# Fox and dilated attention: the 128-column products as three float32r matmuls, and the gate's tokens streamed in turn

## The chip, the cores and the metric

The kernel runs on one core of one Trainium2 chip. The metric is the device time of one execution in microseconds (us), the median of three runs; lower is better.

## What is computed

A decoder trunk of two layers on 256 tokens of width 2048, all in float32. Layer 0 is "forgetting" attention (fox, 16 heads of 128), layer 1 a mixture of three dilated causal windows (8 heads, values of 256); each is followed by a squared-ReLU MLP of width 8192.

```
q = rms_norm(q, q_gain); k = rms_norm(k, k_gain)
c = cumsum(log_sigmoid(h @ w_f + b_f))
s = q @ k.T * scale + c[query] - c[key];  s[key > query] = -inf
o = softmax(s) @ v                       # fox, per head
...
s_g = q_g @ k_g.T * scale - slope * distance * r_g   # dilated, g = 0, 1, 2
o = sum_g exp(s_g - m) @ v / sum_g den_g
x = x + o @ w_out;  x = x + relu(h @ w_up)**2 @ w_down
```

## The kernel before

**Matmuls.** Weights stream from HBM in pieces of 128x1024. ScalarE casts each piece to a float32r "high" part (`wh`, L398) and VectorE subtracts to get the "low" part (`wl`, L399), five pieces ahead at most (`W_BUFS`). Activations are split in the same way. A float32 product is then three float32r matmuls into one PSUM bank: high by high, high by low, low by high (L447 to L449). `in_turn` makes the moving operand alternate between the two halves of a row's columns, element by element; the products that come out are read back through `by_column`.

**Order.** The program is written as one stream: `product_steps` emits the six matmuls of a weight row block and calls `jobs.tick()`, and jobs written as generators (`qk_chain`, `v_chain`, `fox_head`, `dil_head`, `gate_chain`) put their instructions in between; a `yield n` in a job means n steps later. `pin` fixes that order on every engine.

**Attention.** The 256 tokens are two blocks of 128. For queries of block 0 only keys of block 0 count: 128 columns. For block 1 both do: 256 columns. `scores` makes both: for t = 0 one plain float32 matmul of 128 columns on unsplit operands (L797), for t = 1 three float32r matmuls of 256 columns (L800). `pv` multiplies values by the turned probabilities: the values of key block 0 by 256 columns as three float32r matmuls (L749), those of key block 1 by 128 columns as one float32 matmul (L748). `qk_chain` writes q and k with their gains (L707), splits them (L714, L718), and leaves the block-0 queries whole. `v_chain` writes the values (L725, L726) and the low part of block 0's (L728). `p_split` splits the first 256 columns of the probabilities (L775, L777). There are 16 fox heads with one call of `scores` for each t and one step of `pv` each, and 8 dilated heads with three calls of `scores` for each t and two steps of `pv` each.

**The gate.** `gate` multiplies the forget columns (32 stationary columns, high and low) by the normed tokens' high and low parts, 512 contiguous columns, in 16 float32r matmuls (L811), between two projections of layer 0; `gate_chain` reads the sum.

Of the kernel before, what the change touches and what calls it, by code (L numbers as in the profile page):

```python
# [119 lines left out]
def trunk(ctx: ExitStack, tc, x, fox_w_in, fox_b_f, fox_q_gain, fox_k_gain, fox_w_out, dil_w_in,  # L120
# [303 lines left out]
    def halves(t, apart=NC // 2):  # L424
        return t.rearrange("p (b h n) -> p b h n", n=apart, h=2)
# [238 lines left out]
    def qk_chain(acc, tag, key, parts):  # L664
# [35 lines left out]
        yield clear(6)  # L700
        for t in range(NT):
            subs = []
            for n, (c, nh, gcol, (whole, hi, lo)) in enumerate(parts):
                keys = hi.shape[2] == S
                src = qn[t].rearrange("p i (h r) -> p h i r", h=4)[:, c // P:c // P + nh]
                to = sq[0].rearrange("p (n i x) -> p n i x", n=2, i=2)[:, n] if t else whole
                nc.scalar.activation(to.rearrange("p h (i r) -> p h i r", i=4), src, AF.Copy, scale=gain[:, gcol:gcol + 1])  # L707
                if t == 0 and not keys:
                    continue
                at = slice(t * P, (t + 1) * P) if keys else slice(0, P)  # L710

                a, b = (x[:, :, at].rearrange("p i (h n) -> p i h n", h=2) for x in (hi, lo))
                of = to.rearrange("p i (n h) -> p i h n" if keys else "p i (h n) -> p i h n", h=2)
                nc.scalar.copy(a, of)  # L714
                subs.append((b, of, a))
            yield 2
            for b, of, a in subs:
                nc.vector.tensor_sub(b, of, a.bitcast(F32))  # L718
        jobs.done.add(key)

    def v_chain(acc, tag, key, dst):
        yield (tag, "rstd")
        whole, v_hi, v_lo = dst
        by_rstd = [rstd[tag][:, t:t + 1] for t in range(NT)]
        nc.scalar.activation(halves(v_hi), by_column(acc[0]), AF.Copy, scale=by_rstd[0])  # L725
        nc.scalar.activation(halves(whole), by_column(acc[1]), AF.Copy, scale=by_rstd[1])  # L726
        yield 1
        nc.vector.scalar_tensor_tensor(halves(v_lo), by_column(acc[0]), by_rstd[0], halves(v_hi).bitcast(F32),  # L728
                                       ALU.mult, ALU.subtract)
        jobs.done.add(key)  # L730

    oT = {}
# [1 line left out]


    def by_token(po):
        return po[:, 0:S].rearrange("p (n b) -> p b n", b=2)

    def pv(pt_sb, vt, cols, o_hi, o_lo, name, apart):
        for i, c in enumerate(cols):  # L740
            if i:
                yield 1
            po = ps_sc.tile([P, 512], F32, tag="sc", name=f"po_{name}_{i}")
            whole, v_hi, v_lo = vt
            p_hi, p_lo, p_whole = pt_sb
# [4 lines left out]
            hi, lo = (o.rearrange("p (b n) -> p b n", b=2) for o in (o_hi[i], o_lo[i]))  # L750
# [17 lines left out]
        return turned  # L768

    def p_split(turned, name):  # L770
        both = work.tile([P, 2, S], F32R, tag="pT", name=f"pT_{name}", bufs=1)
        p_hi, p_lo = both[:, 0], both[:, 1]
        first = turned.rearrange("p i b r -> p b i r")[:, 0:2]
        hi, lo = (x.rearrange("p (b i r) -> p b i r", b=2, i=4) for x in (p_hi, p_lo))
# [3 lines left out]
        return p_hi, p_lo, turned[:, :, 2, :]  # L778

    def heads_pairs(name, slot):  # L780


        whole = work.tile([P, 2, 2, P], F32, tag=f"qkw{slot}", name=f"{name}w", bufs=1)
        q = work.tile([P, 2, 2, P], F32R, tag=f"q{slot}", name=f"{name}q", bufs=1)
        k = [work.tile([P, 2, S], F32R, tag=f"k{x}{slot + 3}", name=f"{name}k{x}", bufs=1) for x in "hl"]
        return (whole[:, 0], q[:, 0], q[:, 1]), (whole[:, 1], *k)

    def values(name):
        whole = work.tile([P, NC], F32, tag="vw", name=f"{name}w", bufs=1)
# [17 lines left out]
    def gate(tag):  # L807
        pf = ps_sc.tile([2 * FH, 2 * S], F32, tag="sc", name="pf")
        for k in range(KC):
            both = hT[tag][k // 2][:, k % 2]  # L810
            nc.tensor.matmul(pf, wfs[:, k, :], both.rearrange("p x s -> p (x s)"), start=k == 0, stop=k == KC - 1)  # L811
        jobs.spawn(gate_chain(tag, pf))

    def gate_chain(tag, pf):
# [8 lines left out]
        nc.vector.tensor_copy(f, pf[:, 0:S])  # L823
        nc.vector.tensor_add(f, f, pf[:, S:2 * S])
        yield 3
        pft = ps_sc.tile([P, NT, 2 * FH], F32, tag="sc", name="pft")
        for t in range(NT):
            nc.tensor.transpose(pft[:, t, :], f[:, t * P:(t + 1) * P], ident[:2 * FH, :2 * FH])
        z = small.tile([P, NT, FH], F32, tag="g_z", name="g_z", bufs=1)
# [23 lines left out]
        lf = small.tile([P, NT, FH], F32, tag="g_lf", name="g_lf", bufs=1)  # L853
# [468 lines left out]
```

## Time and profile before

| what | value |
|---|---|
| median of 3 runs | 2083.81 us (2083.33 to 2084.59) |
| span of the profiled execution | 2081.4 us |
| PE (TensorE matmul) busy | 2076.2 us, 100% |
| PEld (TensorE weight load) busy | 1819.9 us, 87% |
| DVE (VectorE) busy | 1714.8 us, 82% |
| ACT (ScalarE) busy | 1306.1 us, 63% |
| DMA, mean | 259 GB/s |

The span runs from the first to the last instruction of the profiled execution. Its own device time is not listed apart from the runs; the runs' median is 2.4 us above the span, which is the start and the end that lie outside it. A matmul's row gives its start and its modelled end, through the array's pipeline; what a matmul costs in a stream is therefore the distance from its start to the next one's, not its duration. A plain float32 matmul shows as two records (x2), each with a weight load.

### The profile page before, as it was taken

How to read it: one execution, taken by the hardware profiler on the slowest of the kernel's cores; microseconds unless marked ns; L12 is line 12 of the kernel's file. 1: busy time of each engine (PE TensorE's matmuls, PEld its weight loads, DVE VectorE, ACT ScalarE, POOL GpSimd, SP SyncE). 2: the span in 40 equal slices, each digit the busy share in tenths (PEclk: the TensorE clock that was granted, in tenths of full speed). 3: DMA queues.
4: the chain of work that ended last, by engine and by line, in shares of the span. 5: the costliest groups of instructions: out<-in, count | busy, mean ns of one | idle time of the engine just before them, and what ended most of it. 6: DMA issues, size and time to landing. Idle time of an engine off the chain costs nothing.

```text
span 2081.4 us, 28973 instructions
## 1 busy us (share of the span) xinstructions
PE 2076.2 (100%) x9838; PEld 1819.9 (87%) x9838; DVE 1714.8 (82%) x2183; ACT 1306.1 (63%) x1825; POOL 275.1 (13%) x398
## 2 busy tenths in 40 slices
PE   9999999999999999999999999999999999999999
PEld 7888888888888888888888888888888888888888
DVE  6888876898989889888668787766998898899874
ACT  6665654866666667664656565556766676666662
POOL 2000000111212112120010010000113031212120
PEclk9999999999999999999999999999999999999999
DMA  8888887888988898897877876867888888898885
GB/s 258 257 259 261 262 249 213 268 284 265 270 282 265 263 299 272 264 286 246 281 242 230 250 238 211 262 212 236 269 275 264 279 274 266 276 288 277 263 277 168
DMA packets 357205, 539.04 MB, mean 259 GB/s; under 512 B 43752, under 2 KB 144448, under 8 KB 357056
## 3 DMA queue, kind: packets, MB, share of 16 engines
q1 hardware_dynamic: 334624, 507.41, 76.6%
q0 software_dynamic: 22016, 29.38, 6.2%
q8 instruction: 77, 1.26, 0.2%
q10 hardware_dynamic: 416, 0.39, 0.1%
q14 instruction: 72, 0.59, 0.1%
HBM read 484.09 MB, written 40.39 MB: 252 GB/s over the span
## 4 chain that ended last, share of the span: by engine, by line
PE 98%; DVE 1%; ACT 1%; DMA 1%; issue 0%; SPq 0%; ACTq 0%
PE acc L447 26%; PE acc L448 26%; PE acc L449 26%; PE wide_n_tp L1140 2%; PE wide_n_tp L1141 2%; PE wide_n_tp L1142 2%; PE wide_n_sc L1141 2%; PE wide_n_acc L1140 2%; PE wide_n_sc L1140 2%; PE wide_n_acc L1142 2%; PE wide_n_sc L1142 2%; PE wide_n_acc L1141 2%; PE sc_d L800 0%; DVE wl L399 0%; DMA turned_n<-blocks_n 0%; PE sc_f L800 0%
## 5 line engine op out<-in xcount | busy, mean ns | idle before, releaser
L399 DVE TENSOR_TENSOR wl<-raw,wh 128x1024 fp32r<-128x1024 f32 (+1 forms) x763 | 919.9, 1215 | 302.4 <-ACT wh L398 295.2
L398 ACT CAST wh<-raw 128x1024 fp32r<-128x1024 f32 (+1 forms) x763 | 787.3, 1046 | 498.9 <-PE acc L449 370.1
L447 PE MATMUL acc<-wh,hT_n 128*128 128x512 f32 x1280 | 486.3, 380 | 0.0
L448 PE MATMUL acc<-wl,hT_n 128*128 128x512 f32 x1280 | 485.3, 379 | 0.2 <-DVE wl L399 0.2
L449 PE MATMUL acc<-wh,hT_n 128*128 128x512 f32 x1280 | 485.2, 379 | 0.0
L449 PEld LDWEIGHTS acc<-wh,hT_n 128*128 128x128 f32 x1280 | 241.9, 189 | 34.4 <-DVE hT_n L631 0.2
L448 PEld LDWEIGHTS acc<-wl,hT_n 128*128 128x128 f32 x1280 | 242.1, 189 | 33.7 <-DVE wl L399 0.9
L447 PEld LDWEIGHTS acc<-wh,hT_n 128*128 128x128 f32 x1280 | 242.1, 189 | 33.0 <-ACT hT_n L630 0.2
L447 PE MATMUL acc<-wh,aTh_n1a 128*128 128x512 f32 x512 | 194.0, 379 | 0.0
L448 PE MATMUL acc<-wl,aTh_n1a 128*128 128x512 f32 x512 | 194.0, 379 | 0.0
L449 PE MATMUL acc<-wh,aTl_n1a 128*128 128x512 f32 x512 | 194.0, 379 | 0.0
L447 PE MATMUL acc<-wh,aTh_n3a 128*128 128x512 f32 x480 | 181.9, 379 | 0.0
L448 PE MATMUL acc<-wl,aTh_n3a 128*128 128x512 f32 x480 | 181.9, 379 | 0.0
L449 PE MATMUL acc<-wh,aTl_n3a 128*128 128x512 f32 x480 | 181.9, 379 | 0.0
L996 POOL DMA_DIRECT2D x<-y_n x96 | 84.7, 1325 | 480.0 <-ACT y_n L995 421.1
L398 ACT CAST wh<-sd 128x1024 fp32r<-128x1024 f32 x80 | 84.1, 1051 | 101.9 <-DVE sd L395 78.5
L398 ACT CAST wh<-v 128x1024 fp32r<-128x1024 f32 x80 | 84.1, 1052 | 53.8 <-PE acc L449 41.4
L448 PEld LDWEIGHTS acc<-wl,aTh_n1a 128*128 128x128 f32 x512 | 96.8, 189 | 13.8
L449 PEld LDWEIGHTS acc<-wh,aTl_n1a 128*128 128x128 f32 x512 | 96.8, 189 | 13.7
L447 PEld LDWEIGHTS acc<-wh,aTh_n1a 128*128 128x128 f32 x512 | 96.8, 189 | 13.7
L399 DVE TENSOR_TENSOR wl<-v,wh 128x1024 fp32r<-128x1024 f32 x80 | 97.5, 1218 | 5.8 <-ACT wh L398 4.5
L395 DVE TENSOR_TENSOR sd<-raw,raw 128x1024 f32<-128x1024 f32 x80 | 97.4, 1218 | 5.5 <-DMA raw<-in_mlp_w_up_dram 5.5
(665 smaller groups left out, 3216.8 us busy)
## 6 DMA issues: line engine op xcount, KB each, us to landing
raw<-in_mlp_w_up_dram SPq DMA_DIRECT2D x296, 512.0 KB, 4.9
raw<-in_mlp_w_down_dram SPq DMA_DIRECT2D x256, 512.0 KB, 5.1
raw<-in_dil_w_in_dram SPq DMA_DIRECT2D x192, 256.0 KB, 3.5
raw<-in_fox_w_in_dram SPq DMA_DIRECT2D x94, 512.0 KB, 5.0
raw<-in_fox_w_out_dram SPq DMA_DIRECT2D x32, 512.0 KB, 4.9
raw<-in_dil_w_in_dram SPq DMA_DIRECT2D x32, 512.0 KB, 5.4
raw<-in_dil_w_out_dram SPq DMA_DIRECT2D x32, 512.0 KB, 4.5
x<-y_n POOLq DMA_DIRECT2D x96, 128.0 KB, 6.2
```

Source lines behind the costliest of these rows:

```text
L395: nc.vector.tensor_sub(quarters[0], raw, raws[n - 1][:, 1, :].unsqueeze(1).to_broadcast([P, RAW_SUB, NC]))
L398: nc.scalar.copy(hi[:, part, :], raw[:, part, :])
L399: nc.vector.tensor_sub(lo[:, part, :], raw[:, part, :], hi[:, part, :].bitcast(F32))
L447: nc.tensor.matmul(acc[t], ah[:, tok], hi, start=first, stop=False)
L448: nc.tensor.matmul(acc[t], ah[:, tok], lo, start=False, stop=False)
L449: nc.tensor.matmul(acc[t], al[:, tok], hi, start=False, stop=last)
L996: nc.gpsimd.dma_start(xt[n][:, t, h * HC:h * HC + HC], y, accum_op=ALU.add)
L1140: nc.tensor.matmul(banks[bank], ah, wh, start=what < 3 and of == 0, stop=False, **alone)
L1141: nc.tensor.matmul(banks[bank], ah, wl, start=False, stop=False, **alone)
L1142: nc.tensor.matmul(banks[bank], al, wh, start=False, stop=of == KC // 2 - 1, **alone)
```

## The change

All 72 plain float32 products of 128 columns become three float32r ones each. For this, the block-0 queries and the values of key block 1 are split too, and the probabilities are split over 384 columns instead of 256. The low part of block 1's values lives in tiles that are free in attention (`sd` in fox, the two `bias` tiles in the dilated layer); the queries' low part takes the place of the whole copies. The gate's moving operand alternates between the high and the low part of each token (`p s x` for `p x s`), and its small tiles move into one tile. No `yield` changes.

```
@@ qk_chain @@
-                to = sq[0].rearrange("p (n i x) -> p n i x", n=2, i=2)[:, n] if t else whole
+                to = sq[t].rearrange("p (n i x) -> p n i x", n=2, i=2)[:, n]
-                if t == 0 and not keys:
-                    continue
...
@@ v_chain @@
-        nc.scalar.activation(halves(whole), by_column(acc[1]), AF.Copy, scale=by_rstd[1])
+        nc.scalar.activation(halves(last_hi), by_column(acc[1]), AF.Copy, scale=by_rstd[1])
...
+        for i, lo in enumerate(last_lo):
+            of = slice(i, i + 1) if len(last_lo) > 1 else slice(0, 2)
+            nc.vector.scalar_tensor_tensor(lo.rearrange("p (h n) -> p h n", n=HC), by_column(acc[1])[:, 0, of], by_rstd[1],
+                                           halves(last_hi)[:, 0, of].bitcast(F32), ALU.mult, ALU.subtract)
...
@@ pv @@
-            for v, p, at in ((v_hi, p_hi, 0), (v_hi, p_lo, 1), (v_lo, p_hi, 2)):
-                if at == 2:
-                    nc.tensor.matmul(by_token(po)[:, 1], whole[:, c:c + P], p_whole, start=False, stop=False)
-                nc.tensor.matmul(po[:, 0:S], v[:, c:c + P], p.rearrange("p (b n) -> p n b", b=2), start=at == 0, stop=at == 2)
+            for x, (v, last, p) in enumerate(((v_hi, last_hi[:, c:c + P], p_hi), (v_hi, last_hi[:, c:c + P], p_lo),
+                                              (v_lo, last_lo, p_hi))):
+                nc.tensor.matmul(po[:, 0:S], v[:, c:c + P], in_turn(p[:, 0:S], P // 2), start=x == 0, stop=False)
+                nc.tensor.matmul(po[:, P:S], last, in_turn(p[:, S:S + P], P // 2), start=False, stop=x == 2)
...
@@ p_split @@
-        nc.scalar.copy(hi, first)
+        nc.scalar.copy(hi, blocks)
-        nc.vector.tensor_sub(lo, first, hi.bitcast(F32))
+        nc.vector.tensor_sub(lo, blocks, hi.bitcast(F32))
...
@@ scores @@
-        if t == 0:
-            nc.tensor.matmul(ps[:, 0:P], q_whole[:, i, :], k_whole[:, i, :], start=True, stop=True)
-            return
+        to = ps[:, t * P:(2 * t + 1) * P]
         for x, (a, b) in enumerate(((q_hi, k_hi), (q_hi, k_lo), (q_lo, k_hi))):
-            nc.tensor.matmul(ps[:, P:3 * P], a[:, i, :], in_turn(b[:, i, :], P // 2), start=x == 0, stop=x == 2)
+            nc.tensor.matmul(to, a[:, i, t * P:(t + 1) * P], in_turn(b[:, i, 0:(t + 1) * P], P // 2), start=x == 0, stop=x == 2)
...
@@ gate @@
-            nc.tensor.matmul(pf, wfs[:, k, :], both.rearrange("p x s -> p (x s)"), start=k == 0, stop=k == KC - 1)
+            nc.tensor.matmul(pf, wfs[:, k, :], both.rearrange("p x s -> p s x"), start=k == 0, stop=k == KC - 1)
```

The order on PE at the scores of the first fox head (`sc_f`), before and then changed; `acc` are the projection's matmuls around it:

```order
L449 MATMUL acc_1_918<-wh_880,hT_n_3_238 128x512
L797 MATMUL sc_f_1006<-f_0w 128x128
L800 MATMUL sc_f_1006<-f_0kh,f_0q 128x256
L800 MATMUL sc_f_1006<-f_0kl,f_0q 128x256
L800 MATMUL sc_f_1006<-f_0kh,f_0q 128x256
L447 MATMUL acc_0_917<-wh_899,hT_n_4_261 128x512
```

```order
L449 MATMUL acc_1_918<-wh_879,hT_n_3_239 128x512
L801 MATMUL sc_f_1007<-f_0kh,f_0q 128x128
L801 MATMUL sc_f_1007<-f_0kl,f_0q 128x128
L801 MATMUL sc_f_1007<-f_0kh,f_0qkw 128x128
L801 MATMUL sc_f_1007<-f_0kh,f_0q 128x256
L801 MATMUL sc_f_1007<-f_0kl,f_0q 128x256
L801 MATMUL sc_f_1007<-f_0kh,f_0qkw 128x256
L447 MATMUL acc_0_917<-wh_898,hT_n_4_262 128x512
```

Three float32r matmuls of 128 columns stand where one float32 matmul stood; what comes before and after is the same.

On PE at the first step of `pv` (`po_f`: values of key block 0 are `fv0hl`; of block 1 `fv0w` before, `fv0lh` and `fv0ll` now):

```order
L449 MATMUL acc_1_1130<-wh_1154,hT_n_5_302 128x512
L749 MATMUL po_f_0_1316<-pT_f_1224,fv0hl 128x256 x2
L748 MATMUL po_f_0_1316<-turned_f_1060,fv0w 128x128
L749 MATMUL po_f_0_1316<-pT_f_1224,fv0hl 128x256
L447 MATMUL acc_0_1129<-wh_1174,hT_n_6_331 128x512
```

```order
L449 MATMUL acc_1_1135<-wh_1159,hT_n_5_303 128x512
L751 MATMUL po_f_0_1325<-pT_f_1229,fv0hl 128x256
L752 MATMUL po_f_0_1325<-pT_f_1229,fv0lh 128x128
L751 MATMUL po_f_0_1325<-pT_f_1229,fv0hl 128x256
L752 MATMUL po_f_0_1325<-pT_f_1229,fv0lh 128x128
L751 MATMUL po_f_0_1325<-pT_f_1229,fv0hl 128x256
L752 MATMUL po_f_0_1325<-pT_f_1229,fv0ll_177 128x128
L447 MATMUL acc_0_1134<-wh_1179,hT_n_6_332 128x512
```

The one float32 matmul among three has become three short ones that alternate with the 256-column ones.

On DVE between the values' low part and the keys' low parts of the first fox group, before and then changed:

```order
L399 TENSOR_TENSOR wl_900<-raw_786,wh_899 128x1024
L728 SCALAR_TENSOR_TENSOR fv0hl<-acc_0_716,rstd_n_111,fv0hl 128x512
L399 TENSOR_TENSOR wl_937<-raw_824,wh_936 128x1024
L718 TENSOR_TENSOR f_0kl<-f_0w,f_0kh 128x2x128
L718 TENSOR_TENSOR f_1kl<-f_1w,f_1kh 128x2x128
```

```order
L399 TENSOR_TENSOR wl_899<-raw_783,wh_898 128x1024
L725 SCALAR_TENSOR_TENSOR fv0hl<-acc_0_711,rstd_n_111,fv0hl 128x512
L729 SCALAR_TENSOR_TENSOR fv0ll_177<-acc_1_712,rstd_n_111,fv0lh 128x512
L399 TENSOR_TENSOR wl_938<-raw_823,wh_937 128x1024
L715 TENSOR_TENSOR f_0kl<-sq_('fk', 0)_0_701,f_0kh 128x2x128
L715 TENSOR_TENSOR f_1kl<-sq_('fk', 0)_0_701,f_1kh 128x2x128
```

One more VectorE instruction stands ahead of the next weight piece; the rest keeps its place.

## Rows read from the trace of the kernel before

**Rows 1.** The page: span, and PE's busy time (engine, busy us, share, instructions).
```profile
span 2081.4 us, 28973 instructions
PE 2076.2 (100%) x9838; PEld 1819.9 (87%) x9838; DVE 1714.8 (82%) x2183; ACT 1306.1 (63%) x1825; POOL 275.1 (13%) x398
```

**Rows 2.** The page: shares of the span in the chain that ended last, by engine.
```profile
PE 98%; DVE 1%; ACT 1%; DMA 1%; issue 0%; SPq 0%; ACTq 0%
```

**Rows 3.** Who waited for whom: total us, times, longest us.
```profile
PE acc L448 <- DVE wl L399: 0.2, 1, 0.2
ACT wh L398 <- PE acc L449: 435.0, 312, 2.8
```

**Rows 4.** Timeline of PE at a fox head's scores: start us, duration us, what.
```profile
88.37 0.38 PE L797 MATMUL sc_f<-f_0w 128*128 128x128 f32 x2
88.51 0.36 PE L800 MATMUL sc_f<-f_0kh,f_0q 128*128 128x256 f32 x1
88.70 0.28 PE L800 MATMUL sc_f<-f_0kl,f_0q 128*128 128x256 f32 x1
...
88.92 0.38 PE L447 MATMUL acc<-wh,hT_n 128*128 128x512 f32 x1
```

**Rows 5.** Timeline of PE at a fox head's step of pv.
```profile
116.50 0.38 PE L749 MATMUL po_f<-pT_f,fv0hl 128*128 128x256 f32 x2
116.72 0.39 PE L748 MATMUL po_f<-turned_f,fv0w 128*128 128x128 f32 x2
...
117.06 0.38 PE L447 MATMUL acc<-wh,hT_n 128*128 128x512 f32 x1
```

**Rows 6.** One line of the trace each: the float32 matmuls of 128 columns.
```profile
L797 PE MATMUL sc_f<-f_0w 128*128 128x128 f32 x16 | 3.1, 274 | 0.0
L748 PE MATMUL po_f<-turned_f,fv0w 128*128 128x128 f32 x8 | 1.5, 275 | 0.0
```

**Rows 7.** Timeline of PE and PEld (weight loads) at the gate's running sum: 16 moving columns.
```profile
58.99 0.29 PE L857 MATMUL pc<-g_lf,tri 128*128 128x16 f32 x2
59.10 0.30 PEld L858 LDWEIGHTS pc<-g_lf,ones 128*128 128x128 f32 x2
...
59.32 0.30 PEld L859 LDWEIGHTS pc<-g_lf,tri 128*128 128x128 f32 x2
...
59.55 0.19 PEld L447 LDWEIGHTS acc<-wh,hT_n 128*128 128x128 f32 x1
...
59.66 0.19 PEld L448 LDWEIGHTS acc<-wl,hT_n 128*128 128x128 f32 x1
```

**Rows 8.** Timeline of PE and PEld at two float32 transposes: 16 stationary columns, 128 moving.
```profile
66.13 0.38 PE L864 MATMUL pct<-ident,c_q 128*16 128x128 f32 x2
...
66.24 0.19 PEld L447 LDWEIGHTS acc<-wh,hT_n 128*128 128x128 f32 x1
```

**Rows 9.** Timeline of PE: ten projection matmuls, and the gate's sixteen.
```profile
27.72 0.38 PE L449 MATMUL acc<-wh,hT_n 128*128 128x512 f32 x1
...
29.66 0.38 PE L449 MATMUL acc<-wh,hT_n 128*128 128x512 f32 x1
...
31.55 3.85 PE L811 MATMUL pf<-hT_n,wfs 128*32 128x512 f32 x16
35.24 0.38 PE L447 MATMUL acc<-wh,hT_n 128*128 128x512 f32 x1
```

**Rows 10.** One line of the trace each: splits that grow or multiply (duration ns min/median/max, first and last start).
```profile
L718 DVE TENSOR_TENSOR f_0q<-sq_('fq', 0)_0_515,f_0q x1: 405/405/405, 71.6 to 71.6; 128x256 fp32r<-128x256 f32 x1
L728 DVE SCALAR_TENSOR_TENSOR fv1hl<-acc,rstd_n,fv1hl x1: 742/742/742, 147.4 to 147.4; 128x512 fp32r<-128x512 f32 x1
L777 DVE TENSOR_TENSOR pT_f<-turned_f,pT_f x16: 415/417/421, 114.6 to 330.8; 128x256 fp32r<-128x256 f32 x16
L775 ACT CAST pT_f<-turned_f x16: 396/405/408, 108.8 to 327.6; 128x256 fp32r<-128x256 f32 x16
```

**Rows 11.** Engines' busy us (instructions) by stretch; then granted TensorE clock, DMA share, GB/s.
```profile
66.00:134.00 68.00, 68.00 (x332) 59.89 (x331) 55.90 (x96) 42.97 (x72) 3.28 (x2) 1.00 0.89 274
```

More of the change, by code (lines that the diff above doesn't have):

```diff
@@ L702, in qk_chain @@
             subs = []
-            for n, (c, nh, gcol, (whole, hi, lo)) in enumerate(parts):
-                keys = hi.shape[2] == S
+            for n, (c, nh, gcol, (keys, hi, lo)) in enumerate(parts):
                 src = qn[t].rearrange("p i (h r) -> p h i r", h=4)[:, c // P:c // P + nh]
-                to = sq[0].rearrange("p (n i x) -> p n i x", n=2, i=2)[:, n] if t else whole
+                to = sq[t].rearrange("p (n i x) -> p n i x", n=2, i=2)[:, n]
                 nc.scalar.activation(to.rearrange("p h (i r) -> p h i r", i=4), src, AF.Copy, scale=gain[:, gcol:gcol + 1])
-                if t == 0 and not keys:
-                    continue
-                at = slice(t * P, (t + 1) * P) if keys else slice(0, P)
+                at = slice(t * P, (t + 1) * P)
                 a, b = (x[:, :, at].rearrange("p i (h n) -> p i h n", h=2) for x in (hi, lo))
@@ L722, in v_chain @@
         yield (tag, "rstd")
-        whole, v_hi, v_lo = dst
+        (v_hi, v_lo), (last_hi, last_lo) = dst
         by_rstd = [rstd[tag][:, t:t + 1] for t in range(NT)]
         nc.scalar.activation(halves(v_hi), by_column(acc[0]), AF.Copy, scale=by_rstd[0])
-        nc.scalar.activation(halves(whole), by_column(acc[1]), AF.Copy, scale=by_rstd[1])
+        nc.scalar.activation(halves(last_hi), by_column(acc[1]), AF.Copy, scale=by_rstd[1])
         yield 1
@@ L736, in by_token @@
     def by_token(po):
-        return po[:, 0:S].rearrange("p (n b) -> p b n", b=2)
+        return by_column(po[:, 0:S], P // 2)
     def pv(pt_sb, vt, cols, o_hi, o_lo, name, apart):
@@ L743, in pv @@
             po = ps_sc.tile([P, 512], F32, tag="sc", name=f"po_{name}_{i}")
-            whole, v_hi, v_lo = vt
-            p_hi, p_lo, p_whole = pt_sb
-            for v, p, at in ((v_hi, p_hi, 0), (v_hi, p_lo, 1), (v_lo, p_hi, 2)):
-                if at == 2:
-                    nc.tensor.matmul(by_token(po)[:, 1], whole[:, c:c + P], p_whole, start=False, stop=False)
-                nc.tensor.matmul(po[:, 0:S], v[:, c:c + P], p.rearrange("p (b n) -> p n b", b=2), start=at == 0, stop=at == 2)
-            hi, lo = (o.rearrange("p (b n) -> p b n", b=2) for o in (o_hi[i], o_lo[i]))
+            (v_hi, v_lo), (last_hi, last_lo) = vt
+            apart_lo = NC // len(last_lo)
+            last_lo = last_lo[c // apart_lo][:, c % apart_lo:c % apart_lo + P]
+            p_hi, p_lo = pt_sb
+            for x, (v, last, p) in enumerate(((v_hi, last_hi[:, c:c + P], p_hi), (v_hi, last_hi[:, c:c + P], p_lo),
+                                              (v_lo, last_lo, p_hi))):
+                nc.tensor.matmul(po[:, 0:S], v[:, c:c + P], in_turn(p[:, 0:S], P // 2), start=x == 0, stop=False)
+                nc.tensor.matmul(po[:, P:S], last, in_turn(p[:, S:S + P], P // 2), start=False, stop=x == 2)
+            hi, lo = (halves(o, P // 2) for o in (o_hi[i], o_lo[i]))
             nc.scalar.copy(hi, by_token(po))
@@ L770, in p_split @@
     def p_split(turned, name):
-        both = work.tile([P, 2, S], F32R, tag="pT", name=f"pT_{name}", bufs=1)
+        both = work.tile([P, 2, 3 * P], F32R, tag="pT", name=f"pT_{name}", bufs=1)
         p_hi, p_lo = both[:, 0], both[:, 1]
-        first = turned.rearrange("p i b r -> p b i r")[:, 0:2]
-        hi, lo = (x.rearrange("p (b i r) -> p b i r", b=2, i=4) for x in (p_hi, p_lo))
-        nc.scalar.copy(hi, first)
+        blocks = turned.rearrange("p i b r -> p b i r")
+        hi, lo = (x.rearrange("p (b i r) -> p b i r", b=3, i=4) for x in (p_hi, p_lo))
@@ L776, in p_split @@
+        nc.scalar.copy(hi, blocks)
         yield 2
-        nc.vector.tensor_sub(lo, first, hi.bitcast(F32))
-        return p_hi, p_lo, turned[:, :, 2, :]
+        nc.vector.tensor_sub(lo, blocks, hi.bitcast(F32))
+        return p_hi, p_lo
     def heads_pairs(name, slot):
-        whole = work.tile([P, 2, 2, P], F32, tag=f"qkw{slot}", name=f"{name}w", bufs=1)
-        q = work.tile([P, 2, 2, P], F32R, tag=f"q{slot}", name=f"{name}q", bufs=1)
+        q = [work.tile([P, 2, S], F32R, tag=f"{of}{slot}", name=f"{name}{of}", bufs=1) for of in ("q", "qkw")]
@@ L785, in heads_pairs, with values @@
         k = [work.tile([P, 2, S], F32R, tag=f"k{x}{slot + 3}", name=f"{name}k{x}", bufs=1) for x in "hl"]
-        return (whole[:, 0], q[:, 0], q[:, 1]), (whole[:, 1], *k)
-    def values(name):
-        whole = work.tile([P, NC], F32, tag="vw", name=f"{name}w", bufs=1)
+        return (False, *q), (True, *k)
+    def values(name, of, bufs):
+        last_hi = work.tile([P, NC], F32R, tag="vw", name=f"{name}lh", bufs=1)
+        last_lo = [work.tile([P, NC // bufs], F32R, tag=of, name=f"{name}ll{i}", bufs=bufs) for i in range(bufs)]
@@ L790, in values @@
         both = work.tile([P, 2, NC], F32R, tag="v", name=f"{name}hl", bufs=1)
-        return whole, both[:, 0], both[:, 1]
+        return (both[:, 0], both[:, 1]), (last_hi, last_lo)
     def scores(ps, t, q, k, i):
-        (q_whole, q_hi, q_lo), (k_whole, k_hi, k_lo) = q, k
-        if t == 0:
-            nc.tensor.matmul(ps[:, 0:P], q_whole[:, i, :], k_whole[:, i, :], start=True, stop=True)
-            return
+        (_, q_hi, q_lo), (_, k_hi, k_lo) = q, k
+        to = ps[:, t * P:(2 * t + 1) * P]
@@ L822, in gate_chain @@
         f = work.tile([2 * FH, S], F32, tag="s", name="g_f", bufs=S_BUFS)
-        nc.vector.tensor_copy(f, pf[:, 0:S])
-        nc.vector.tensor_add(f, f, pf[:, S:2 * S])
+        parts = pf.rearrange("p (s x) -> p x s", x=2)
+        nc.vector.tensor_copy(f, parts[:, 0])
+        nc.vector.tensor_add(f, f, parts[:, 1])
         yield 3
+        gates = work.tile([P, 7, NT, FH], F32, tag="t2", name="gates")
         pft = ps_sc.tile([P, NT, 2 * FH], F32, tag="sc", name="pft")
@@ L828, in gate_chain @@
             nc.tensor.transpose(pft[:, t, :], f[:, t * P:(t + 1) * P], ident[:2 * FH, :2 * FH])
-        z = small.tile([P, NT, FH], F32, tag="g_z", name="g_z", bufs=1)
+        z, neg, e, u, u2, s, lf = (gates[:, i] for i in range(7))
         for t in range(NT):
@@ L833, in gate_chain @@
             nc.vector.scalar_tensor_tensor(z[:, t, :], pft[:, t, FH:2 * FH], r, z[:, t, :], ALU.mult, ALU.add)
-        neg = small.tile([P, NT, FH], F32, tag="g_n", name="g_n", bufs=1)
         nc.vector.tensor_scalar(neg, z, -1.0, None, ALU.mult)
         nc.vector.tensor_tensor(neg, neg, z, ALU.min)
-        e = small.tile([P, NT, FH], F32, tag="g_e", name="g_e", bufs=1)
         nc.scalar.activation(e, neg, AF.Exp)
         yield 1
-        u = small.tile([P, NT, FH], F32, tag="g_u", name="g_u", bufs=1)
         nc.vector.tensor_scalar(u, e, 2.0, None, ALU.add)
@@ L844, in gate_chain @@
         nc.vector.tensor_mul(u, e, u)
-        u2 = small.tile([P, NT, FH], F32, tag="g_u2", name="g_u2", bufs=1)
         nc.vector.tensor_mul(u2, u, u)
-        s = small.tile([P, NT, FH], F32, tag="g_s", name="g_s", bufs=1)
         nc.vector.tensor_scalar(s, u2, 1.0 / 19.0, None, ALU.mult)
@@ L852, in gate_chain @@
         nc.vector.tensor_scalar(z, z, 0.0, None, ALU.min)
-        lf = small.tile([P, NT, FH], F32, tag="g_lf", name="g_lf", bufs=1)
         nc.vector.scalar_tensor_tensor(lf, s, -2.0, z, ALU.mult, ALU.add)
@@ L965, in dilated @@
             qTs, kTs = zip(*(heads_pairs(f"d{q4}_{g}", g) for g in range(3)))
-            vt = values(f"dv{q4}")
+            vt = values(f"dv{q4}", "bias", 2)
             def heads_post(g):
@@ L1267, in trunk @@
         qT, kT = zip(*(heads_pairs(f"f{j}_{i}", i) for i in range(2)))
-        vt = values(f"fv{j}")
+        vt = values(f"fv{j}", "sd", 1)
         product(keys_h(tag), lhs_h(tag), lambda acc: qk_chain(
```

## The prediction

> **What bounds it now.** I read the page first: PE is busy for 2076.2 of 2081.4 us [rows 1], and PE makes up 98% of the chain that ended last [rows 2]. So what counts is how long PE's stream is. The waits say whether anything feeds PE too late: it waits for VectorE's low part of a weight piece 0.2 us in all, while ScalarE waits 435.0 us for PE to give a weight buffer back [rows 3]. The splits run ahead of PE as far as their five buffers let them; every microsecond added to PE's stream is a microsecond of time, and a little more work on VectorE and ScalarE is not.
>
> The stage in question is attention. In the timeline, the reader is to see distances from start to start. At a fox head's scores [rows 4] one float32 matmul of 128 columns (two records) starts at 88.37, three float32r matmuls of 256 columns follow, and the projection goes on at 88.92: 0.55 us for five records, 0.11 each. From 88.70, the second float32r matmul, to 88.92 are two records in 0.22, so 0.11 for each float32r of 256 columns, and 0.55 - 3 x 0.11 = 0.22 for the float32 one. A step of pv is the same again: 116.50 to 117.06, five records of 0.112 [rows 5]. A projection's matmul of 512 columns takes (29.66 - 27.72) / 9 = 0.2156 [rows 9], so a float32r column streams in 0.42 ns at the full granted clock (1.00 in this stage [rows 11]), and 128 of them would stream in 0.054.
>
> **Part 1: the short products.** Removed: 40 float32 products in scores (five groups of 16 records, two records a product) and 32 in pv (eight groups of 8) [rows 6], 72 x 0.22 = 15.8 us. Added: 216 float32r matmuls of 128 columns with a weight load of their own each. No row shows such a matmul, so I bound it.
>
> - From below: 0.054 us, streaming alone, were the weight load hidden.
> - From above: 0.22 us, what the float32 product of the same size takes now [rows 4].
> - Between them: the weight load. At the gate's running sum, matmuls have 128 stationary and only 16 moving columns, so hardly anything streams. Yet from the first start at 58.99 to the load at 59.66 six loads go by, 0.11 us apart [rows 7]: 59.10 (two), 59.32 (two), 59.55, 59.66. The last interval, 59.55 to 59.66, is a float32r load (L447's) behind a 16-column matmul, and L448's load can't start before it is over.
>
> I take 0.11: rows 7 are the nearest, since there too a load of 128 stationary columns stands behind a matmul too short to hide it, and one of these loads is float32r. Then a short matmul costs as much as one of 256 columns, three in place of two records: +0.11 us a product. In scores, six slots in place of five, 40 x 0.11 = 4.4 us; in pv, six in place of five, 32 x 0.112 = 3.6 us. Together **+8.0 us**, all on the path, since PE has no gaps there (68.00 of 68.00 us busy [rows 11]).
>
> Here the Trainium skill would give another price. TensorE: Matmul & The Clock Gate, section Back-to-back issue gap, puts a sustained stream of load and matmul pairs at about 81 ns for 128 columns; by it the sum would be an estimate of 72 x (0.243 - 0.22) = +1.7 us. The same section has 131 ns for 512 columns, where this trace has 215.6 [rows 9], so its figures don't describe this stream, and the sum above goes by the rows.
>
> **Part 2: the gate.** Its 16 matmuls of 512 contiguous columns take 35.24 - 31.55 = 3.69 us, 0.2306 each; the projection's, which alternate between two places 256 columns apart, take 0.2156 [rows 9]. After the change the gate's operand alternates too. I take the projection's rate: 16 x 0.015 = **-0.24 us**. If the difference comes from its 32 stationary columns instead, it is 0. The Trainium skill speaks against this edit: SBUF — State Buffer, section on the DMA port swizzle, says that successive accesses run at full rate within a 16-byte line and pay at each change of line. By it the gate would get slower, not faster; the rows just read have the alternating stream the faster one. Either way it is under 0.02% of the time.
>
> **Part 3: VectorE and ScalarE.** VectorE gets 20 subtractions of 256 columns for the queries (8 in fox, 12 dilated), at 0.405 each; the low part of block 1's values, 4 x 0.742 in fox and 8 halves at some 0.4 in the dilated layer; and 24 splits of the probabilities grow from 256 to 384 columns, by half of 0.417 at most [rows 10]. That is 8.1 + 3.0 + 3.2 + 5.0 = 19.3 us at most, over eight groups of heads: about 2.4 us a group. ScalarE gets 20 casts at about 0.405 and 24 longer ones, 8.1 + 4.9 = 13 us. I cost both at **nothing**: a stretch of 68 us over a fox group has VectorE busy 55.9 and ScalarE 43.0 [rows 11], so 12 us stay free on VectorE for 2.4 more, and the weight buffers are full ahead of PE. What the cover is worth if it goes: up to 19.3 us. No `yield` changes, so every instruction keeps its place among the steps, DMAs and PE's order included; nothing is moved past SP's or POOL's queue. Waits: a longer probability split delays pv by 0.2 us at most, with 1.5 us between its end (114.6 + 0.4) and the matmul that needs it (116.50) [rows 5, 10].
>
> **Sum.** 8.0 - 0.24 + 0 = +7.7 us (0.11 each is read to about 2%). The span of 2081.4 becomes 2089.1; the median of the runs is 2.4 above this execution's span, so 2083.8 + 7.7 = **2091.5 us**, 0.37% slower. About 0.2%, 4.2 us, is what a measurement of this kernel can tell from no change.
>
> **The rivals.**
>
> 1. **The loads hide (faster).** Float32r loads may go quicker in a row than behind a float32 matmul. [...] With 0.054, the sum is 72 x (0.162 - 0.22) = -4.2, with the gate -4.4: 2079.4 us. The rule that points here is in the Trainium skill, TensorE: Matmul & The Clock Gate, section Weight-path perf modes: weights load four at a time when there are 128 and the type isn't FP32. Against it: the loads of L447 and L448, float32r, are 0.19 us long each, and a float32 pair with 0.11 between its starts is 0.30 long, so 0.19 each as well [rows 7]; no quick load shows. Chance 0.06, two thirds of it beyond 0.2%.
> 2. **Short float32r loses its rate (much slower).** Two float32 transposes of 128 columns with 16 stationary columns, whose loads are short, still start 0.11 apart (66.13, then the next load at 66.24 as the second starts) [rows 8]: float32 streams at half rate and needs two passes. Every float32r matmul in the trace has 256 or 512 columns. If a shorter one falls back to float32's 0.22, the change costs 72 x (0.66 - 0.22) = +31.7, with the gate 2115.3 us. Nothing speaks for it but that no row excludes it. Chance 0.07.
> 3. **VectorE falls behind.** In the attention stages it goes from 82% busy to about 86%; a late low part of a weight piece stops PE at L448. If a third of the 19.3 us gets through, 2098 us; all of it, 2111. For it: a low part can be made only behind ScalarE's cast, which gets more work too. Against: ScalarE waits 435.0 us for PE [rows 3]. Chance 0.05.
> 4. **The load costs less than 0.11 in a mixed stream**, near the break-even of 0.073 to 0.085 us: 72 x (0.24 - 0.22) = +1.4, 2085 us, no change that can be told. Chance 0.04.
>
> **Numbers.** The forecast, a load of 0.11 us for each short matmul with VectorE hidden, has 0.78. Its own range is 2089 to 2093; I widen it to 2087.5 below (a load of 0.10 with the gate's gain: 72 x 0.08 - 0.24 = +5.5 would be 2089.3, and some offset between runs) and to 2097 above, which takes in the milder half of rival 3. That leaves out about 0.19. Faster by over 0.2%: two thirds of rival 1, 0.04. Within 0.2%: the rest of it and rival 4, 0.06. Slower: 0.90.
>
> **What would show it.** In the trace after: scores take 0.66 us from the first short matmul to the projection's next instead of 0.55, and pv 0.67 instead of 0.56; weight loads 0.11 apart within them. 0.49 in scores would be rival 1, about 0.99 rival 2. The gate's 16 matmuls take 3.45 instead of 3.69 us. PE's waits for L399 stay under 2 us in all; if they rise to 5 or more, rival 3. The prediction is wrong if three short matmuls don't cost 0.33 us.

## The result, and the profile after

The changed kernel takes 2093.89 us (median of 5 runs, 2092.64 to 2094.95), the kernel before 2083.98 (5 runs, 2083.33 to 2084.59) in the same comparison: +9.9 us, a ratio of 1.0049 with a 95% interval of 1.0036 to 1.0061, which is 7.5 to 12.7 us. The forecast was 2091.5 in a range of 2087.5 to 2097.

The page of the changed kernel, with the lines that answer to [rows 1, 2]:

```profile
span 2092.2 us, 29211 instructions
PE 2085.1 (100%) x9910; PEld 1827.3 (87%) x9910; DVE 1730.3 (83%) x2215; ACT 1315.1 (63%) x1845; POOL 275.2 (13%) x398
...
PE 95%; DMA 2%; ACT 1%; DVE 1%; issue 0%; POOL 0%; SPq 0%; ACTq 0%; DVEq 0%; POOLq 0%
```

PE is still what bounds it; its busy time grew by 8.9 us, the span by 10.8. The records grew by 72: 216 new ones in place of 144. The timeline of PE at the first fox head's scores (start us, duration us, what), beside [rows 4]:

```profile
89.53 0.22 PE L801 MATMUL sc_f<-f_0kh,f_0q 128*128 128x128 f32 x1
89.58 0.28 PE L801 MATMUL sc_f<-f_0kl,f_0q 128*128 128x128 f32 x1
89.70 0.28 PE L801 MATMUL sc_f<-f_0kh,f_0qkw 128*128 128x128 f32 x1
89.81 0.33 PE L801 MATMUL sc_f<-f_0kh,f_0q 128*128 128x256 f32 x1
...
90.20 0.38 PE L447 MATMUL acc<-wh,hT_n 128*128 128x512 f32 x1
```

From 89.53 to 90.20 are 0.67 us where the kernel before had 0.55. The weight loads of the same stretch show the beat (PEld):

```profile
89.53 0.19 PEld L801 LDWEIGHTS sc_f<-f_0kl,f_0q 128*128 128x128 f32 x1
89.64 0.19 PEld L801 LDWEIGHTS sc_f<-f_0kh,f_0qkw 128*128 128x128 f32 x1
89.75 0.19 PEld L801 LDWEIGHTS sc_f<-f_0kh,f_0q 128*128 128x128 f32 x1
89.86 0.19 PEld L801 LDWEIGHTS sc_f<-f_0kl,f_0q 128*128 128x128 f32 x1
```

One load every 0.11 us, through the short matmuls and the 256-column ones alike. A step of pv, beside [rows 5], and the gate, beside [rows 9]:

```profile
118.11 0.27 PE L751 MATMUL po_f<-pT_f,fv0hl 128*128 128x256 f32 x1
118.22 0.22 PE L752 MATMUL po_f<-pT_f,fv0lh 128*128 128x128 f32 x1
118.28 0.33 PE L751 MATMUL po_f<-pT_f,fv0hl 128*128 128x256 f32 x1
...
118.72 0.43 PE L447 MATMUL acc<-wh,hT_n 128*128 128x512 f32 x1
119.00 0.38 PE L448 MATMUL acc<-wl,hT_n 128*128 128x512 f32 x1
```
```profile
32.95 3.62 PE L812 MATMUL pf<-hT_n,wfs 128*32 128x512 f32 x16
36.40 0.38 PE L447 MATMUL acc<-wh,hT_n 128*128 128x512 f32 x1
```

In pv, the record of the projection's next matmul starts at 118.72, while the last short one still streams; the one behind it starts at 119.00. Counted back from there by one matmul of 512 columns (0.216), the six records end at 118.78: 0.67 us. The gate takes 3.45 us where it took 3.69.

**Where the time came from.** Both programs run the same 9408 projection and MLP matmuls in the same order, so the start of each can be subtracted between two traces, and the lag read stretch by stretch. The two profiled executions differ by 10.8 us, of which:

| stretch (us of the kernel before) | lag gained, us |
|---|---|
| opening, to 14 | +1.40 |
| to the end of the gate, 35 | -0.24 |
| fox, 35 to 357 | +3.58 |
| hand-over to the first MLP, to 401 | +0.33 |
| first MLP | 0.0 |
| dilated layer, to 1417 | +4.47 |
| hand-over to the second MLP, to 1503 | +1.28 |
| the rest | 0.0 |

The products are fox and dilated, 8.05 us. The opening and the hand-overs, 3.0 us together, were not forecast. (A hand-over is where a layer's output projection ends and the MLP begins.) In the first 14 us no instruction is changed; there the fourth block of transposes waits for tokens:

```profile
12.38 0.66 PE L626 MATMUL ptx_n<-ident,x 128*128 128x128 f32 x4 [0.83 <-DMA x<-in_x_dram]
```

At the second hand-over PE waits twice for VectorE's low part of a weight piece (in brackets, the idle time before and who ended it; the weight loads' own waits there are 0.74 and 0.58 us):

```profile
1465.82 0.48 PE L448 MATMUL acc<-wl,hT_n 128*128 128x512 f32 x1 [0.34 <-DVE wl L399]
...
1468.86 0.48 PE L448 MATMUL acc<-wl,hT_n 128*128 128x512 f32 x1 [0.18 <-DVE wl L399]
```

### The profile page after: what moved, and what is told of

The parts are those of the page before. It is cut to its first block, busy times and chain, and to the rows that moved or that the text cites. A ratio compares the mean times of both kernels' runs of the same rounds, so it can differ in the third digit from the quotient of the medians.

```text
span 2092.2 us, 29211 instructions
## 1 busy us (share of the span) xinstructions
PE 2085.1 (100%) x9910; PEld 1827.3 (87%) x9910; DVE 1730.3 (83%) x2215; ACT 1315.1 (63%) x1845; POOL 275.2 (13%) x398
## 3 DMA queue, kind: packets, MB, share of 16 engines
q8 instruction: 78, 1.28, 0.3%
## 4 chain that ended last, share of the span: by engine, by line
PE 95%; DMA 2%; ACT 1%; DVE 1%; issue 0%; POOL 0%; SPq 0%; ACTq 0%; DVEq 0%; POOLq 0%
PE acc L447 25%; PE acc L448 25%; PE acc L449 25%; PE wide_n_tp L1139 2%; PE wide_n_tp L1138 2%; PE wide_n_tp L1137 2%; PE wide_n_sc L1138 2%; PE wide_n_acc L1138 2%; PE wide_n_acc L1139 2%; PE wide_n_sc L1139 2%; PE wide_n_sc L1137 2%; PE wide_n_acc L1137 2%; DMA raw<-in_mlp_w_up_dram 1%; PE sc_d L801 1%; PE sc_f L801 1%; ACT wh L398 1%
## 5 line engine op out<-in xcount | busy, mean ns | idle before, releaser
L399 DVE TENSOR_TENSOR wl<-raw,wh 128x1024 fp32r<-128x1024 f32 (+1 forms) x763 | 920.0, 1214 | 295.8 <-ACT wh L398 283.8
L449 PEld LDWEIGHTS acc<-wh,aTl_n3a 128*128 128x128 f32 x480 | 90.7, 189 | 12.9
```

Of the source, the lines that this page charges most:

```text
L399: nc.vector.tensor_sub(lo[:, part, :], raw[:, part, :], hi[:, part, :].bitcast(F32))
L449: nc.tensor.matmul(acc[t], al[:, tok], hi, start=False, stop=last)
```

## The experiments

Theory A is that a matmul takes the longer of its own stream and the next one's weight load, 0.11 us for 128 stationary columns. Theory B, its rival, is that a float32r matmul under 256 columns streams at half rate, which would give 0.107 us for 128 columns too. Beside them stands the question whose the other 3 us are: the further splits', the longer attention's, or no one's but the execution's.

**The two kernels again.** No edit; a second trace of each.

> The kernel before once more, for a second trace of it. The changed kernel's profiled execution is 1.4 us late by the 14th us, before any changed instruction. If that is what executions differ by (the time at which the tokens land), this trace's opening differs from the first one's by a like amount, and the hand-over at some 1450 us by some tenths; if the change causes it, this one agrees with the first to 0.2 us.

> The changed kernel once more, for a second trace of it. If the late opening is scatter, its first projection matmul behind the fourth token block comes anywhere between 11.5 and 13 us; if the change causes it, at 12.8 again. The products should cost 72 x 0.11 = 8.0 us as in the first trace; the waits at the hand-over to the second MLP (1.3 us in the first trace) are there again if they belong to the change.

One run each: the kernel before 2084.86 us (2083.25 in another run beside it), the changed one 2092.15. The second trace of the kernel before lags the first by 0.48 us after the opening and by 1.74 at the end, all of it gained by the end of the first MLP; in the changed one's the opening gained 0.25 where it had gained 1.40. So the opening is scatter, and the first profile of the kernel before was an early one. The products cost 8.2 us this time (3.76 and 4.47). At the first hand-over the second trace of the kernel before gained 0.39, as much as the changed ones (0.33 and 0.32): scatter as well. At the second hand-over it gained nothing, the changed kernel 0.77.

**The gate alone.**

```
-            nc.tensor.matmul(pf, wfs[:, k, :], both.rearrange("p x s -> p (x s)"), start=k == 0, stop=k == KC - 1)
+            nc.tensor.matmul(pf, wfs[:, k, :], both.rearrange("p x s -> p s x"), start=k == 0, stop=k == KC - 1)
...
```

> Only the gate's moving operand alternates; all else as in the kernel before. If the order in which the operand streams is what costs, its 16 matmuls take 3.45 us from the first start to the projection's next (0.2157 each) where the kernel before has 3.69; if the 32 stationary columns cost it, 3.69 as before. Time: 0 to 0.24 us less, not to be told from no change. The opening (first 14 us) should be as before up to what executions differ by.

2084.0 us against 2083.99, a ratio of 0.9997 (0.9988 to 1.0007): no change that can be told. The timeline of its gate:

```profile
31.77 3.62 PE L811 MATMUL pf<-hT_n,wfs 128*32 128x512 f32 x16
35.22 0.38 PE L447 MATMUL acc<-wh,hT_n 128*128 128x512 f32 x1
```

3.45 us, as expected if the order of the stream costs.

**Each group of products alone.** In the first, the values' products and in the second the scores' (with their splits) are put back to what they were before; the gate is as before in both. The lines are shown against the changed kernel.

For the scores alone:

```
...
-                nc.tensor.matmul(po[:, P:S], last, in_turn(p[:, S:S + P], P // 2), start=False, stop=x == 2)
...
+                    nc.tensor.matmul(by_token(po)[:, 1], whole[:, c:c + P], p_whole, start=False, stop=False)
...
```

For pv alone:

```
...
+        if t == 0:
+            nc.tensor.matmul(ps[:, 0:P], q_whole[:, i, :], k_whole[:, i, :], start=True, stop=True)
+            return
...
```

> Only the 40 products of the scores go as three float32r matmuls (with the queries' split that this needs); the values' products and the gate as before. By the weight-load theory each product costs 0.11 us more: 40 x 0.11 = +4.4 us on PE, about 2088.4 us. By a rival in which the extra splits on VectorE and ScalarE cost, more than that, with waits of PE for them.

> Only the 32 products of values and probabilities go as three float32r matmuls (with the splits that this needs); scores and gate as before. Weight-load theory: 32 x 0.11 = +3.6 us, about 2087.6 us. Together with the scores alone and the gate this should make up the 8 us that the change costs on PE; what the change has above that (2 us) would then be waits.

The scores alone: 2089.84 us, ratio 1.0027 (1.0018 to 1.0037), +5.85 us; of the lag of its trace 2.33 + 2.68 = 5.0 us lie in the two attention stages, and 1.32 at the second hand-over. Pv alone: 2087.53, ratio 1.0014 (1.0005 to 1.0024), +3.5 us; 1.81 + 1.79 = 3.6 in the stages, 0.69 at the hand-over. The stages give what 40 and 32 times 0.11 ask for (the fox stage of the scores alone holds 0.5 us more than 16 x 0.11: one wait of PE, 0.58 us on its weight load at 210.86, for the low part of the probabilities, whose split is unchanged there; in the second trace of the kernel before, one wait at 89.71 for the keys' low part adds 0.62 with no change at all). Most of what is above it in the scores alone, and what its time has above the 4.4 us expected, sits at the hand-over.

**What sets a short matmul's time.** Rows of 16 equal matmuls behind the gate, with S stationary and M moving columns, each closed by one of 512 columns.

```
+        for name, held, moving in cases:
...
+            to = ps_sc.tile([P, 512], F32, tag="sc", name=name)
+            for x in range(16):
+                w = held[x % len(held)]
...
+                nc.tensor.matmul(to[0:m, 0:n], w, moving, start=True, stop=True)
+            nc.tensor.matmul(to, full, by_turns, start=True, stop=True)
```

> The kernel before with eleven rows of 16 equal matmuls behind the gate's, each followed by one of 512 columns; S stationary and M moving columns. Theory A, a matmul takes the longer of its own stream (0.42 ns a column) and the next one's weight load (0.11 us for S=128): pa S=128 M=128 0.11 each; pb S=32 M=128 0.055; pc S=128 M=64 0.11; pd S=128 M=256 0.11; pe S=128 and 32 in turn, M=128, 0.08 on average. Theory B, a short float32r matmul streams at half rate: pa 0.11, pb 0.11, pc 0.055, pe 0.11. For the gate: pg S=32, 512 contiguous, and ph S=128, 512 contiguous, against pi and pj with the same streamed in turn: 0.23 and 0.23 against 0.216 and 0.216 if the order costs; 0.23, 0.216, 0.23, 0.216 if the few stationary columns do. Float32, pk S=128 M=128 and pl S=32 M=128: two records of 0.11 each in both, if float32 streams at half rate by itself; 0.055 in pl if the load sets it.

The timeline of PE (L834 the sixteen, L835 the one that closes them):

```profile
35.16 1.89 PE L834 MATMUL pa<-hT_n,hT_n 128*128 128x128 f32 x16
36.89 0.43 PE L835 MATMUL pa<-hT_n,hT_n 128*128 128x512 f32 x1
37.39 1.08 PE L834 MATMUL pb<-hT_n,hT_n 128*32 128x128 f32 x16
38.30 0.43 PE L835 MATMUL pb<-hT_n,hT_n 128*128 128x512 f32 x1
41.22 1.97 PE L834 MATMUL pc<-hT_n,hT_n 128*128 128x64 f32 x16 [2.48 <-DVE g_f L847]
43.02 0.46 PE L835 MATMUL pc<-hT_n,hT_n 128*128 128x512 f32 x1
...
46.82 1.59 PE L834 MATMUL pe<-hT_n,hT_n 128*128 128x128 f32 x16
48.25 0.43 PE L835 MATMUL pe<-hT_n,hT_n 128*128 128x512 f32 x1
```

Distances divided by 16: pa, 128 by 128, 0.108 us; pb, the same stream with 32 stationary columns, **0.057**; pc, 64 moving columns behind 128 stationary, **0.112**; pe, 128 and 32 stationary in turn, 0.089. Half the moving columns cost the same, a quarter of the stationary ones half: it is the stationary side that sets the time, and theory B, which wanted pb at 0.11 and pc at 0.055, is out. (Fewer stationary columns also mean fewer rows of output. That it is the load and not the output is argued, from load records that follow one another every 0.11 us, and not tested apart.) In pe the pair, 0.18, is one load of 128 columns and one short stream, with its first matmuls still at a lower clock; from 47.19 on its starts lie 0.056 and 0.111 apart in turn. Pd is read for its first four starts alone, 43.32 to 43.66: 0.11 apart, as theory A asks for 256 columns. Its others come at half the clock, 0.21 apart: PE had waited 2.48 us up to 41.22 and then ran the short pc, and from 44.0 to 46.4 the granted clock was 0.50, the lower level (1.2 GHz), as the stretches show (PE, PEld, DVE, ACT, POOL busy us; granted clock; DMA):

```profile
44.00:46.40 2.40, 2.40 (x14) 2.40 (x13) 0.00 (x0) 0.00 (x0) 0.00 (x0) 0.50 0.00 0
46.90:48.20 1.30, 1.30 (x17) 1.30 (x16) 0.00 (x0) 0.00 (x0) 0.00 (x0) 0.92 0.00 0
48.50:52.00 3.50, 3.50 (x16) 1.63 (x15) 0.00 (x0) 0.00 (x0) 0.00 (x0) 1.00 0.00 0
```

The gate's cause, and float32, from the rows further on:

```profile
48.52 3.88 PE L834 MATMUL pg<-hT_n,hT_n 128*32 128x512 f32 x16
52.24 0.38 PE L835 MATMUL pg<-hT_n,hT_n 128*128 128x512 f32 x1
52.45 3.81 PE L834 MATMUL ph<-hT_n,hT_n 128*128 128x512 f32 x16
56.10 0.38 PE L835 MATMUL ph<-hT_n,hT_n 128*128 128x512 f32 x1
56.32 3.62 PE L834 MATMUL pi<-hT_n,hT_n 128*32 128x512 f32 x16
59.77 0.38 PE L835 MATMUL pi<-hT_n,hT_n 128*128 128x512 f32 x1
...
63.66 3.73 PE L834 MATMUL pk<-hT_n,hT_n 128*128 128x128 f32 x32
67.15 0.46 PE L835 MATMUL pk<-hT_n,hT_n 128*128 128x512 f32 x1
67.54 3.68 PE L834 MATMUL pl<-hT_n,hT_n 128*32 128x128 f32 x32
71.15 0.48 PE L835 MATMUL pl<-hT_n,hT_n 128*128 128x512 f32 x1
```

Contiguous streams take 3.72 / 16 = 0.233 with 32 stationary columns and 3.65 / 16 = 0.228 with 128; in turn 3.45 / 16 = 0.216. So it is the order. Float32 takes 3.49 / 32 = 0.109 a record with 128 stationary columns and 3.61 / 32 = 0.113 with 32; the ends of the rows differ, and between starts within them it is 0.112 and 0.109. With 32 stationary columns no long load is there to set it: it is the stream, at half the rate, which happens to be about as long as a load.

**The short matmuls' moving operand contiguous.**

```
-            nc.tensor.matmul(to, a[:, i, t * P:(t + 1) * P], in_turn(b[:, i, 0:(t + 1) * P], P // 2), start=x == 0, stop=x == 2)
+            moving = in_turn(b[:, i, 0:2 * P], P // 2) if t else b[:, i, 0:P]
+            nc.tensor.matmul(to, a[:, i, t * P:(t + 1) * P], moving, start=x == 0, stop=x == 2)
...
```

> The changed kernel with the 216 short matmuls' moving operand contiguous instead of in turn (the columns of these products come out in another order). If the weight load sets their time, what they stream is hidden and nothing changes: 0.67 us from the first of the scores to the projection's next, about 2093.9 us. If streaming sets it, they get slower by a few per cent of 0.11.

2092.55 us in one run, within the changed kernel's runs (2092.15 to 2094.95); the dilated stage gained 4.47 us, to the hundredth what it gained in both traces of the changed kernel. (Fox gained 4.07, again with one wait for the keys' low part, at 88.91.) What a short matmul streams is hidden under the load.

**The splits without the products.** The changed kernel with its 72 products as one float32 matmul each, on the high parts, first in turn, then contiguous:

```
+        if t == 0:
+            nc.tensor.matmul(to, q_hi[:, i, 0:P].bitcast(F32), in_turn(k_hi[:, i, 0:P], P // 2).bitcast(F32), start=True, stop=True)
+            return
...
```

and then, against that:

```
-            nc.tensor.matmul(to, q_hi[:, i, 0:P].bitcast(F32), in_turn(k_hi[:, i, 0:P], P // 2).bitcast(F32), start=True, stop=True)
+            nc.tensor.matmul(to, q_hi[:, i, 0:P].bitcast(F32), k_hi[:, i, 0:P].bitcast(F32), start=True, stop=True)
...
```

> All of the changed kernel's splits on VectorE and ScalarE and its gate, but the 72 products as one float32 matmul each, on the high parts alone (the low parts are left out of these products). If the splits are hidden, 2083.9 less 0.24 us for the gate: about 2083.7. If they cost what the change has above 8 us, 2085 to 2086, with waits of PE where the dilated layer hands over to the MLP (some 1450 us) of about 1.3 us as in the changed kernel.

> The changed kernel's splits and gate, the 72 products as one float32 matmul each on the high parts (low parts left out of these products), now with the moving operand contiguous (so that columns come out in another order), since in turn a float32 product took 0.27 us and not 0.22. If contiguous float32 is back at 0.22, the scores take 0.55 us from the first to the projection's next. If the further splits cause the waits at the hand-over, 0.4 to 1.3 us there and about 2084.5 us in all; if attention's length does, none there and about 2083.8.

The first was a miss: 2087.78 us, ratio 1.0016 (1.0006 to 1.0025), more than either reading gave it. Its timeline says why:

```profile
89.68 0.43 PE L803 MATMUL sc_f<-f_0kh,f_0q 128*128 128x128 f32 x2
...
90.28 0.38 PE L447 MATMUL acc<-wh,hT_n 128*128 128x512 f32 x1
```

0.60 us for the scores, not 0.55: in turn, a float32 product takes 0.27 us and not 0.22, and 72 of them add 3.4 us (1.49 in fox and 1.87 in the dilated stage); the second hand-over gained 0.44. The experiment had moved PE as well as the splits. Contiguous, from 88.00 to 88.56, they are back:

```profile
88.00 0.39 PE L803 MATMUL sc_f<-f_0kh,f_0q 128*128 128x128 f32 x2
...
88.56 0.38 PE L447 MATMUL acc<-wh,hT_n 128*128 128x512 f32 x1
```

Then the kernel takes 2084.85 us, ratio 1.0002 (0.9992 to 1.0011): all the further splits cost nothing that can be told. In its trace fox and the dilated stage gain 0.00 us each, and the second hand-over 0.24.

**Attention longer without the splits.** The kernel before with one 256-column matmul done twice in each product:

```
+            nc.tensor.matmul(po[:, 0:S], v_hi[:, c:c + P], p_hi.rearrange("p (b n) -> p n b", b=2), start=True, stop=True)
...
+        nc.tensor.matmul(ps[:, P:3 * P], q_hi[:, i, :], in_turn(k_hi[:, i, :], P // 2), start=True, stop=True)
```

> The kernel before with one float32r matmul of 256 columns more for each of the 72 products (the first of its group done twice, the first result overwritten), and nothing else: no further splits, the gate as before. By the slot theory every matmul with 128 stationary columns costs 0.11 us whatever it streams up to 256 columns, so 72 x 0.11 = +8.0 us, as in the changed kernel: about 2092.0 us. At the hand-over from the dilated layer to the second MLP: if PE's waits there (0.8 to 1.3 us in the changed kernel, none in the kernel before) come from the further splits, none here; if they come from attention taking PE longer, 0.4 to 1.3 us here too.

2093.24 us, ratio 1.0044 (1.0029 to 1.0059), +9.2 us. Fox gains 3.57 and the dilated stage 4.47: a whole extra matmul of 256 columns costs as much as three short float32r matmuls cost over the float32 one. The second hand-over gains 0.40. So a kernel with none of the further splits is as much slower as the changed one, within the two intervals.

**The hand-over, put together.** The traces follow the wait back to where it starts. First the kernel before: a low part of a weight piece while the dilated layer's output projection still runs, ScalarE's wait for the turned tokens (`turned_n`) that a DMA brings, its cast of a later weight piece, and the low part that PE takes at the place of the second wait, the one that all eight waiting traces share.

```profile
1433.32 1.23 DVE L399 TENSOR_TENSOR wl<-raw,wh 128x1024 fp32r<-128x1024 f32 x1 [1.36 <-ACT wh L398]
1434.57 0.40 ACT L552 ACTIVATE room_n<-turned_n,gain 128x128 f32<-128x128 f32 x1 [1.28 <-DMA turned_n<-blocks_n]
...
1439.83 1.04 ACT L398 CAST wh<-raw 128x1024 fp32r<-128x1024 f32 x1 [0.28 <-DMA raw<-in_mlp_w_up_dram]
...
1456.74 1.23 DVE L399 TENSOR_TENSOR wl<-raw,wh 128x1024 fp32r<-128x1024 f32 x1 [1.15 <-ACT wh L398]
...
1458.02 0.19 PEld L448 LDWEIGHTS acc<-wl,hT_n 128*128 128x128 f32 x1
```

The same in the changed kernel, up to the cast:

```profile
1442.84 1.23 DVE L399 TENSOR_TENSOR wl<-raw,wh 128x1024 fp32r<-128x1024 f32 x1 [1.36 <-ACT wh L398]
1445.17 0.40 ACT L552 ACTIVATE room_n<-turned_n,gain 128x128 f32<-128x128 f32 x1 [2.35 <-DMA turned_n<-blocks_n]
...
1450.67 1.05 ACT L398 CAST wh<-raw 128x1024 fp32r<-128x1024 f32 x1 [0.55 <-DVE hT_n L557]
```

The low part at 1433.32 comes at 1442.84, 9.52 us later, which is exactly PE's own lag there. So VectorE isn't late by then, with all its further splits behind it, and in each of the eleven traces compared it keeps step with PE to 0.01 us at this place. ScalarE's cast, at 1439.83 and 1450.67, is 10.84 later, 1.32 more than PE's lag. In between lies the wait for the DMA, 2.35 us instead of 1.28. The kernel before has no room for that: its low part is done at 1457.97 and PE's load of it starts at 1458.02, a cover of 0.05 us. By trace:

| trace | the cast later than PE's lag, us | gained at the hand-over, us |
|---|---|---|
| the kernel before | 0.00 | 0.00 |
| the same, second trace | -0.39 | 0.00 |
| the gate alone | -0.08 | 0.00 |
| the changed kernel | 1.32 | 1.28 |
| the same, second trace | 0.80 | 0.77 |
| the scores alone | 1.37 | 1.32 |
| pv alone | 0.74 | 0.69 |
| short operand contiguous | 0.64 | 0.61 |
| splits alone, in turn | 0.48 | 0.44 |
| splits alone, contiguous | 0.27 | 0.24 |
| attention longer | 0.33 | 0.40 |

What PE waits is the lateness of this cast, to 0.1 us, and the cast is late because DMAs land late against PE: the turned tokens, and in most of the traces the weight piece itself. Why they do isn't shown. The three traces with attention as it was have no wait and the eight others have one, so it probably comes with the change; but the landing moves by 0.45 us among those three (ScalarE's wait is 0.83 to 1.28), and the scores alone waited longer than the whole change did in its second trace.

## Why the prediction was right, point by point

- **The short products, +8.0 us: right.** They cost 3.58 + 4.47 = 8.05 us in the first trace, in six slots for five, as read from loads behind 16-column matmuls [rows 7]. The probe shows what the choice between the bounds rested on: the stationary side sets the time, as a load does (0.112 with 64 columns, 0.057 with 32 stationary ones).
- **The Trainium skill's figure** of about 81 ns for pairs of load and matmul at 128 columns (TensorE: Matmul & The Clock Gate, Back-to-back issue gap) would have given an estimate of +1.7 us; the probe has 0.108 us for such pairs in float32r, and the measurement decides.
- **The gate, -0.24 us: right.** 3.69 to 3.45 us, and the order of the stream is its cause, shown with 32 and with 128 stationary columns. The rule of 16-byte lines in the Trainium skill (SBUF — State Buffer, the DMA port swizzle) would have it the other way round; here the measurement decides.
- **Splits hidden: right.** VectorE's busy time grew by 15.5 us and ScalarE's by 9.0, against at most 19.3 and 13 forecast; alone they cost nothing that can be told, and VectorE keeps step with PE up to the second hand-over.
- **The step that failed: "Waits".** It priced a longer probability split and nothing else, and took the DMAs to keep their place against PE because no `yield` changed. At the second hand-over they don't: ScalarE's cast comes 1.32 and 0.80 us late behind them, and PE waits 1.28 and 0.77 us that were not in the sum. The cover had been read in a fox group (12 us free on VectorE [rows 11]); at the hand-over it was 0.05 us. The check named for it, PE's waits for L399, hardly shows this (0.7 us in the whole trace), since the weight loads wait first: 0.74 and 0.58 us there, and 2.8 in the whole trace, where the two traces of the kernel before have 0.9 and 1.9, all of them elsewhere.
- **The sum, +7.7 for a measured +9.9.** The products and the gate give 7.8 of it, the hand-over 0.8 to 1.3. What is left is of the size by which single traces differ: the two of the kernel before end 1.74 us apart. That 2093.89 lies in the range is in part luck: the forecast's own range, 2089 to 2093, misses it, and the upper bound had been widened for a VectorE that falls behind. One figure under the sum was misread, without harm to it: a run takes 1.7 us more than its own span (2093.89 for 2092.2), so some 0.7 of the 2.4 us was that the profiled execution was quicker than the median.
- **The rivals.** Hidden loads are out (a 64-column matmul takes 0.112). The half rate of short float32r is out (0.057 at 32 stationary columns). VectorE falling behind under its further splits is out: it keeps step to 0.01 us until ScalarE waits for the DMA, and then loses about 1 us, not 6 or more. A cheaper load is out (one every 0.11 us in the mixed stream of the scores).

The gate alone is the only part worth keeping. Its 0.24 us shows in the trace; in the time it can't be told from the kernel before, and no version here beats that.

## What to carry to other kernels

On PE count slots, not columns: a matmul lasts as long as the longer of its own stream and the next one's weight load, here 0.11 us behind 128 stationary columns, the time of 256 float32r columns. Three float32r matmuls take three slots, none shorter than a load, so 0.33 us at least; one float32 one takes two records, each streamed at half the rate. At 128 columns the three lose, 0.33 for 0.22. At 256 columns they should win, 0.33 for 0.44; that is an estimate from 0.109 us for a float32 record of 128 columns, and no run here has one of 256. Cover is to be read at every stage, and not at the busiest alone: here it was 12 us in a fox group and 0.05 us at a hand-over, where a DMA that landed 1 us late went straight into the time. And before a small difference is laid to a change, a second trace of the unchanged kernel tells which stretches move by themselves.

## What was not expected of the hardware

The order in which the moving operand is read works one way for float32r and the other way for float32. In turn between two places, 512 float32r columns take 0.216 us instead of 0.228 to 0.233 contiguous, while a float32 product of 128 columns takes 0.27 us in turn instead of 0.22. No run here tells why. And after a wait of PE of 2.5 us followed by 16 matmuls of 64 columns, the granted clock stood at half for 2.4 us and more, in the one execution that has this.
